# A two-layer decoder trunk on one core: the gate/up products with four of eight chunks by sevens, two of the sums on GpSimd

## The chip, the cores and the metric

The kernel runs on one NeuronCore of a Trainium2 chip. Its engines work side by side: TensorE (PE; its weight loads are listed as PEld), VectorE (DVE), ScalarE (ACT), GpSimd (POOL) and SyncE (SP, here only a queue that starts transfers). The metric is the device time of one execution in microseconds; the times given are medians of several runs.

## The reference

The input is x with 256 tokens of 2048 float32 channels. Two layers follow each other, each a token mixer and a feed-forward network, both behind an RMSNorm and both added to the stream:

```python
for i in range(DEPTH):                      # DEPTH = 2
    hn = rmsnorm(h, norm_mix[i])
    if i % N_MIXERS == 0:
        mix = pool_mixer(hn, pool_w[j], pool_scale[j])
    else:
        mix = diff_attention(hn, w_qkv[j], ..., w_o[j], lambda_init)
    h = h + mix
    h = h + swiglu(rmsnorm(h, norm_ffn[i]), w_gate[i], w_up[i], w_down[i])
return rmsnorm(h, final_norm)
```

The pooling mixer takes, in four groups of 512 channels, the mean over the last 2, 4, 8 or 16 tokens less the token itself, times a 512x512 matrix. The attention has 8 heads of two score maps each. `swiglu` is `(silu(h @ wg) * (h @ wu)) @ wd` with 5632 inner channels. Everything is float32, and nearly all of the arithmetic lies in the matrix products with the weights, 353 MB of which are read once.

## The kernel before

**Products in three terms.** A float32 product is made of fp32r matmuls: each operand is split into a high half (a cast) and a low half (what the cast left), and a product is high x high, high x low and low x high. For weights, `halves` (lines 111 to 116) casts on ScalarE (`whi`, L114) and subtracts on VectorE (`wlo`, L115). The activations are the stationary operand, 128x128; the weights are the moving one, 512 columns.

**A group.** `group` (lines 137 to 178) makes one product of the 256 tokens with 1024 columns of a weight matrix. It goes through the input channels in chunks of 256; a weight chunk is four blocks of 128x512 in one tile of 1 MB, loaded by `load` (L108, SyncE's queue, three buffers `raw`), split into three pairs of buffers `whi`/`wlo`. A chunk is a product of 2x2 blocks. Done plainly it has eight block products, 24 matmuls, into the four banks of the result. Done by sevens (Strassen's scheme in Winograd's form) it has seven block products, 21 matmuls, into seven banks, and needs sums of the blocks: `sums` (lines 118 to 124) makes T1 and T3 (L120), T2 (L122) and T4 (L123) on VectorE, `sum_halves` splits them on ScalarE (L129) and VectorE (L130). The tiles of the sums have one buffer each. Plain chunks of the same group add into the banks M2, P3, P4 and X, which are combined later.

**Which chunks go by sevens** is listed per stage: `SEVEN = (2, 4, 6)` for gate/up, `SEVEN_DOWN` for the down product, `SEVEN_QKV`, `SEVEN_O`. The first gate/up group of layer 0 takes only chunk 6. The eight PSUM banks are M1, M6, M7, P5, P3, P4, M2, X (0 to 7). `combined` (lines 180 to 197) makes the four result blocks out of them with two copies on ScalarE and eight additions on VectorE, the last of them reading X (L196).

**The feed-forward network** (`ffn`, lines 388 to 451) has 11 gate/up groups of eight chunks in three bundles (4, 4, 3); after each bundle come two down groups (8, 8 or 6 chunks) that add to `x_tok`. After a gate/up group come silu (L408), the product with up (L409), and `pair` (lines 230 to 253), which transposes the result on TensorE (L235) into an auxiliary bank, one of 0 to 3 in turn (`aux`), and splits it; where the pair feeds a chunk by sevens, it also makes the sums S1 to S4.

**The start** (lines 264 to 385): x is loaded in four pieces of 512 KB (two column halves for each half of the tokens), the four mixer weights and the band matrix behind them on SyncE's queue. For each group g, `turned` transposes and scales x (L310, L313, L315), `product` multiplies with the weights as full float32 (L322), `scaled_halves`, `means` and `residual` make the windowed means and add them, `onward` transposes the new stream for the next product.

**The end**: the last down group, all plain, is followed for each half of the tokens by the addition (L429), squares (L216), a product with the final gain (L435), 1/sqrt (`rsqrt`), scaling (L445, L446) and the output (L447).

**Order.** The order on each engine isn't that of the source: a scheduler of the framework puts every instruction where its operands and buffers are free by its own model of time; the waits between engines follow from it. So matmuls of the next group stand between the transposes of the last one. SyncE's queue starts its transfers one after another, and a load that waits for a buffer holds those behind it.

Of the kernel before, what the change touches and what calls it, by code (L numbers as in the profile page):

```python
# [30 lines left out]
BAND = 3 * P  # L31
LAMBDA_INIT = 0.8 - 0.6 * math.exp(-0.3)
# [6 lines left out]
SEVEN = (2, 4, 6)  # L39
# [12 lines left out]
def trunk_kernel(ctx, tc, x_n, gains, scale_in, final_in, subln, lam_in, band, dist,  # L52
# [31 lines left out]
    dist_sb = const.tile([P, 2 * P], F32, name="dist_sb")  # L84
    ident = const.tile([P, P], F32, name="ident")
    ones = const.tile([P, P], F32, name="ones")
    nc.vector.memset(ones, 1.0)
    make_identity(nc, ident)

# [28 lines left out]
    def sums(pool, raw):  # L118
        t = pool.tile([P, 4, 512], F32, name="tsum")
        nc.vector.tensor_tensor(t[:, T1:T3 + 1], raw[:, B11:B22 + 1],  # L120
                                raw[:, B12:B12 + 1].broadcast_to([P, 2, 512]), ALU.add)
        nc.vector.tensor_tensor(t[:, T2], t[:, T1], raw[:, B22], ALU.add)  # L122
        nc.vector.tensor_tensor(t[:, T4], t[:, T2], raw[:, B21], ALU.add)  # L123
        return t
# [12 lines left out]
    def group(steps, pool):  # L137


        plan = []  # L140
        for a, seven, src in steps:
            if seven:
                plan.append([(M1, [(A11, 0, B11)]), (M2, [(A12, 0, B21)]), (M6, [(S2, 1, T2)]), (M7, [(S3, 1, T3)]),
                             (P5, [(S1, 1, T1)]), (P3, [(S4, 0, B22)]), (P4, [(A22, 1, T4)])])
            else:
                plan.append([(C11, [((0, 0), 0, B11), ((1, 0), 0, B21)]), (C12, [((0, 0), 0, B12), ((1, 0), 0, B22)]),
                             (C21, [((0, 1), 0, B11), ((1, 1), 0, B21)]), (C22, [((0, 1), 0, B12), ((1, 1), 0, B22)])])
        left = {}
# [4 lines left out]
        for (a, seven, src), step in zip(steps, plan):  # L153
            raw = load(src)
            t = sums(pool, raw) if seven else None
            w = [halves(raw, B11 if seven else 0)]
            if seven:
                w.append(sum_halves(pool, t))
            for b, parts in step:
                first = b not in ps  # L160
                if first:
                    ps[b] = bank(b)
                for at, which, block in parts:
                    hi, lo = w[which]
                    if seven:
                        ah, al = a[:, 0, at], a[:, 1, at]
                    else:
                        k, t = at
                        if a.shape[2] == 8:
                            slot = ((A11, A21), (A12, A22))[k][t]  # L170
                            ah, al = a[:, 0, slot], a[:, 1, slot]
                        else:
                            ah, al = (a[:, k, i, t * P:(t + 1) * P] for i in range(2))
                    for x, y in ((ah, hi), (ah, lo), (al, hi)):
                        left[b] -= 1
                        nc.tensor.matmul(ps[b], x, y[:, block], start=first, stop=(left[b] == 0))  # L176
                        first = False
        return ps
# [51 lines left out]
    def pair(dst, src, gains, seven):  # L230

        ps = aux((P, 2, 2, P))
# [32 lines left out]
    with tc.tile_pool(name="start", bufs=1, reuse_waits="tile") as st:  # L265

        warm = tmp.tile([P, 8], F32, name="warm", bufs=1)
        nc.scalar.activation(warm[:, 0:1], ones[:, 0:1], AF.Sqrt)
# [4 lines left out]
        w_pool = [st.tile([P, 4, 512], F32, name=f"w{g}") for g in range(3)]  # L273
        scale_sb = st.tile([P, D], F32, name="scale_sb")
        band_raw = st.tile([P, 4 * BAND + 8], F32, name="band_raw")
        nc.scalar.dma_start(out=gain_sb, in_=gains)
        ss_in = tmp.tile([P, 2, 4], F32, name="ss")

        def load_x(i):
            cols = slice(i * 1024, (i + 1) * 1024)  # L280
            for t in range(2):
                nc.sync.dma_start(out=x_tok[:, t, cols], in_=x_n[:, t, cols])

        def squares(i):
            for t in range(2):
                sq = st.tile([P, 1024], F32, name="sq_in")
                nc.scalar.activation(sq, x_tok[:, t, i * 1024:(i + 1) * 1024], AF.Square, accum_out=ss_in[:, t, i:i + 1])
# [10 lines left out]
        counts = band_raw[:, 4 * BAND:].rearrange("p (g t) -> p g t", t=2)  # L298
        xt, yp, y, zp = {}, {}, {}, {}

        def turned(g):

            xt[g] = [st.tile([P, 2, S], F32, name="xt", bufs=6) for _ in range(2)]
            for i in range(2):
                ps = aux((P, 2, S))
                for k in range(2):
                    at = 2 * i + k
                    cols = slice((4 * g + at) * P, (4 * g + at + 1) * P)
                    for t in range(2):
                        nc.tensor.transpose(ps[:, k, t * P:(t + 1) * P], x_tok[:, t, cols], ident)  # L310
# [6 lines left out]
        def product(g):  # L317

            yp[g] = [bank(4 + 2 * (g % 2) + t) for t in range(2)]
            for at in range(4):  # L320
                for t in range(2):
                    nc.tensor.matmul(yp[g][t], xt[g][at // 2][:, at % 2, t * P:(t + 1) * P], w_pool[g][:, at],  # L322
                                     start=(at == 0), stop=(at == 3))
# [30 lines left out]
        turned(0)  # L354
        squares(0)
        turned(1)
        product(0)
        squares(1)
        tot = tmp.tile([P, 2], F32, name="ss_tot")
# [15 lines left out]
        product(3)  # L375
# [10 lines left out]
    nc.sync.dma_start(out=dist_sb, in_=dist)  # L386

    def ffn(layer, xq, ss, next_op, next_gain):
# [3 lines left out]
        with tc.tile_pool(name=f"ffn{layer}", bufs=1, reuse_waits="tile") as hp:  # L392
            g0 = 0
            ys = []
            for c, n in enumerate(CHUNKS):
# [6 lines left out]
                for g in range(g0, g0 + n):  # L402

                    by_seven = SEVEN[-1:] if g == 0 and layer == 0 else SEVEN
# [5 lines left out]
                    for i in range(2):  # L410
                        at = 2 * (g - g0) + i
                        ht = hp.tile(pair_shape(at in SEVEN_DOWN), F32R, name="h", tag=f"h{at}")
                        pair(ht, lambda k, t: cs[t][1][:, (2 * i + k) * P:(2 * i + k + 1) * P], None, at in SEVEN_DOWN)
                        hp_tiles.append(ht)
                for o in range(2):
                    if last and o == 1:
# [5 lines left out]
                    by_seven = () if last and o and next_op is None else SEVEN_DOWN  # L422
                    cs = combined(group([(hp_tiles[i], i in by_seven, w_down[layer][o, 2 * g0 + i])
                                         for i in range(2 * n)], hp), hp)
                    ends = last and o and next_op is None
                    for b, t in ((0, 0), (1, 0), (0, 1), (1, 1)) if ends else ((0, 0), (0, 1), (1, 0), (1, 1)):
# [5 lines left out]
                        if last and next_op is None:  # L432
                            if b == 0 and t == 0:
                                ys.append(hp.tile([P, 2, 2, 512], F32, name="y", tag=("tsum", "thi")[o]))
# [4 lines left out]
                        if ends and b:  # L439

                            tot = tmp.tile([P, 2], F32, name="ss_tot")
                            nc.vector.tensor_reduce(tot[:, 0:1], ss_next[:, t], AX.X, ALU.add)
                            rt = rsqrt(tot[:, 0:1], D, 1)
                            for i in range(2):
                                nc.scalar.activation(ys[i][:, t, 0], ys[i][:, t, 0], AF.Copy, scale=rt)  # L445
                                nc.vector.tensor_scalar(ys[i][:, t, 1], ys[i][:, t, 1], rt, None, ALU.mult)  # L446
                                (nc.scalar if i else nc.sync).dma_start(  # L447
                                    out=out[t * P:(t + 1) * P, i * 1024:(i + 1) * 1024],
                                    in_=ys[i][:, t].rearrange("p b n -> p (b n)"))
# [8 lines left out]
    with tc.tile_pool(name="attn", bufs=1, reuse_waits="tile") as ap_, ExitStack() as heads:  # L458
# [4 lines left out]
            small[:, a:b] for a, b in ((0, 2), (2, 4), (4, 8), (8, 10), (10, 12), (12, 13), (14, 16)))  # L463
        nc.sync.dma_start(out=subln_sb, in_=subln)
# [3 lines left out]

        nc.vector.tensor_tensor(lp, lam_sb[:, 0:2], lam_sb[:, 2:4], ALU.mult)
# [75 lines left out]
        for g in range(2):  # L545
            cs = scaled(combined(group([(xp[p], p in SEVEN_QKV, w_v[g, p]) for p in range(NP)], op_), op_), (r_col, r_col))
            for h in range(4 * g, 4 * g + 4):
# [13 lines left out]
                oT[h] = op_.tile(pair_shape(h in SEVEN_O), F32R, name=f"oT{h}")  # L561
# [33 lines left out]
def _constants():  # L595
# [14 lines left out]
    band = np.concatenate([band.reshape(P, -1), counts.reshape(P, -1)], axis=1)  # L610
# [50 lines left out]
```

## Time and profile before

| What | us |
|---|---|
| median of three runs (lowest, highest) | 1848.4 (1846.57, 1849.46) |
| the profiled execution, its own time | 1848.95 |
| its span in the trace | 1847.2 |
| ScalarE busy in the span | 1034.5 |
| VectorE busy in the span | 1595.1 |

The span runs from the first to the last recorded instruction or transfer; the 1.75 us around it are in the execution's time alone. Rows of groups read: line, engine, operation, result<-operands, shapes, count | busy us, mean ns | idle time before. In rows of stretches each engine has its busy time and, in brackets, its number of instructions; the granted TensorE clock, the share of the DMA engines and their GB/s end the row. Durations of successive VectorE instructions overlap by about 0.08 us, since a row's time includes its start-up; busy time counts the overlap once.

### The profile page before, as it was taken

Reading aid. Unit: us, or ns where it says so; the run is one execution under the profiler, and the core shown is the slowest. Engines: PE = TensorE matmul, PEld = TensorE weight load, DVE = VectorE, ACT = ScalarE, POOL = GpSimd, SP = SyncE. Lnnn points to the kernel's source line nnn. Section 1 sums busy time; section 2 is a strip of 40 time slices with the busy share of each in tenths; the row PEclk is TensorE's granted clock in tenths of the full one; section 3 lists DMA queues with packets and bytes.
Section 4 is the critical chain, followed back from the end, with each engine's and each line's share of the span. In section 5 each row is a group of like instructions: output and inputs, shape, how many; then the busy total and the mean of one; then the engine's idle time right before and its main releaser. Section 6 shows DMA issues by size and latency. Waiting matters only on the chain.

```text
span 1847.2 us, 20836 instructions
## 1 busy us (share of the span) xinstructions
PE 1832.2 (99%) x8194; PEld 1493.6 (81%) x8194; DVE 1595.1 (86%) x1644; ACT 1034.5 (56%) x998; POOL 0.7 (0%) x6
## 2 busy tenths in 40 slices
PE   9999999999999999999999999999999999999997
PEld 5888888888888888888888888788888888888886
DVE  5889998898989899988888678998989899988985
ACT  5655555555554556665566655555554555555553
POOL 0000000000000000000000000000000000000000
PEclk9999999999999999999999999999999999999999
DMA  6555555555555555555554454555555555566552
GB/s 256 198 193 194 186 212 196 208 200 192 203 198 205 202 186 182 206 181 175 170 179 160 162 193 169 208 202 188 203 201 205 197 190 190 211 217 210 197 198 99
DMA packets 50210, 356.74 MB, mean 193 GB/s; under 512 B 5952, under 2 KB 6080, under 8 KB 7488
## 3 DMA queue, kind: packets, MB, share of 16 engines
q1 hardware_dynamic: 49392, 353.27, 54.2%
q10 hardware_dynamic: 720, 2.15, 0.3%
q8 instruction: 64, 1.05, 0.2%
q14 instruction: 34, 0.28, 0.0%
HBM read 353.30 MB, written 2.10 MB: 192 GB/s over the span
## 4 chain that ended last, share of the span: by engine, by line
PE 94%; DVE 3%; DMA 1%; ACT 1%; issue 1%; SPq 0%; DVEq 0%; ACTq 0%
PE b L176 89%; PE b L235 2%; PE b L322 2%; DVE wlo L115 1%; PE b L506 1%; PE b L536 0%; DMA w<-pool_w 0%; ACT whi L114 0%; DMA raw<-w_v 0%; DMA raw<-w_gu 0%; DVE tsum L120 0%; DVE tlo L130 0%; PE b L310 0%; PE b L491 0%; ACT sq L216 0%
## 5 line engine op out<-in xcount | busy, mean ns | idle before, releaser
L176 PE MATMUL b<-whi,xp 128*128 128x512 f32 x2824 | 909.3, 392 | 1.0 <-DVE c L188 1.0
L114 ACT CAST whi<-raw 128x1536 fp32r<-128x1536 f32 (+1 forms) x328 | 581.3, 1773 | 583.1 <-PE b L176 498.7
L115 DVE TENSOR_TENSOR wlo<-raw,whi 128x1536 fp32r<-128x1536 f32 (+1 forms) x328 | 692.6, 2112 | 193.9 <-ACT whi L114 193.7
L176 PEld LDWEIGHTS b<-whi,xp 128*128 128x128 f32 x2824 | 528.3, 188 | 110.5 <-DVE c L188 1.4
L176 PE MATMUL b<-wlo,xp 128*128 128x512 f32 x1412 | 551.8, 391 | 0.0
L176 PE MATMUL b<-whi,h 128*128 128x512 f32 x1108 | 354.5, 390 | 0.0
L176 PEld LDWEIGHTS b<-wlo,xp 128*128 128x128 f32 x1412 | 265.3, 188 | 53.6
L130 DVE TENSOR_TENSOR tlo<-tsum,thi 128x2048 fp32r<-128x2048 f32 x108 | 246.8, 2285 | 5.8 <-ACT thi L129 5.8
L176 PEld LDWEIGHTS b<-whi,h 128*128 128x128 f32 x1108 | 207.4, 188 | 43.1
L176 PE MATMUL b<-wlo,h 128*128 128x512 f32 x554 | 215.8, 389 | 0.0
L129 ACT CAST thi<-tsum 128x2048 fp32r<-128x2048 f32 x108 | 206.2, 1909 | 16.7 <-DVE tsum L123 16.6
L176 PE MATMUL b<-thi,xp 128*128 128x512 f32 x608 | 211.8, 390 | 0.0
L120 DVE TENSOR_TENSOR tsum<-raw 128x1024 f32<-128x1024 f32 x108 | 131.8, 1220 | 2.6 <-DMA raw<-w_v 1.1
L176 PEld LDWEIGHTS b<-thi,xp 128*128 128x128 f32 x608 | 113.9, 188 | 24.1 <-ACT thi L129 0.9
L176 PEld LDWEIGHTS b<-wlo,h 128*128 128x128 f32 x554 | 104.0, 188 | 21.3
L176 PE MATMUL b<-tlo,xp 128*128 128x512 f32 x304 | 119.5, 393 | 0.0
L176 PE MATMUL b<-thi,h 128*128 128x512 f32 x240 | 83.7, 389 | 0.0
L123 DVE TENSOR_TENSOR tsum<-tsum,raw 128x512 f32<-128x512 f32 x108 | 74.3, 688 | 2.2
L122 DVE TENSOR_TENSOR tsum<-tsum,raw 128x512 f32<-128x512 f32 x108 | 74.0, 685 | 0.7
L176 PE MATMUL b<-whi,oT 128*128 128x512 f32 x236 | 74.4, 392 | 0.0
L176 PEld LDWEIGHTS b<-tlo,xp 128*128 128x128 f32 x304 | 57.0, 188 | 16.0 <-DVE tlo L130 4.4
L176 PEld LDWEIGHTS b<-thi,h 128*128 128x128 f32 x240 | 45.0, 188 | 9.2
(139 smaller groups left out, 1181.6 us busy)
## 6 DMA issues: line engine op xcount, KB each, us to landing
raw<-w_gu SPq DMA_DIRECT2D x176, 1024.0 KB, 4.9
raw<-w_down SPq DMA_DIRECT2D x88, 1024.0 KB, 4.9
raw<-w_qk SPq DMA_DIRECT2D x32, 1024.0 KB, 4.8
raw<-w_v SPq DMA_DIRECT2D x16, 1024.0 KB, 4.8
raw<-w_o SPq DMA_DIRECT2D x16, 1024.0 KB, 4.9
w<-pool_w SPq DMA_DIRECT2D x3, 1024.0 KB, 11.7
x_tok<-x_n SPq DMA_DIRECT2D x4, 512.0 KB, 6.1
scale_sb<-scale_in SPq DMA_DIRECT2D x1, 1024.0 KB, 13.1
```

The costliest lines, as they stand in the source:

```text
L114: nc.scalar.copy(hi[:, lo_block:], raw[:, lo_block:])
L115: nc.vector.tensor_tensor(lo[:, lo_block:], raw[:, lo_block:], f32(hi[:, lo_block:]), ALU.subtract)
L120: nc.vector.tensor_tensor(t[:, T1:T3 + 1], raw[:, B11:B22 + 1], raw[:, B12:B12 + 1].broadcast_to([P, 2, 512]), ALU.add)
L122: nc.vector.tensor_tensor(t[:, T2], t[:, T1], raw[:, B22], ALU.add)
L123: nc.vector.tensor_tensor(t[:, T4], t[:, T2], raw[:, B21], ALU.add)
L129: nc.scalar.copy(hi, t)
L130: nc.vector.tensor_tensor(lo, t, f32(hi), ALU.subtract)
L176: nc.tensor.matmul(ps[b], x, y[:, block], start=first, stop=(left[b] == 0))
L235: nc.tensor.transpose(ps[:, i, 1 - t if seven else t], src(i, t), ident)
L322: nc.tensor.matmul(yp[g][t], xt[g][at // 2][:, at % 2, t * P:(t + 1) * P], w_pool[g][:, at], start=(at == 0), stop=(at == 3))
L506: nc.tensor.matmul(sc[:, :nk], qk[:, 0, c, qb * P:(qb + 1) * P], qk[:, 1, c, :nk], start=True, stop=True)
```

## The change

- `SEVEN` becomes `(0, 2, 4, 6)`. Group 0 of layer 0 still has only chunk 6 by sevens and group 0 of layer 1 still 2, 4, 6; the other 20 gate/up groups have four.
- `sums` makes T2 and T4 on GpSimd, in every stage that uses sevens.
- The pairs of h are transposed into bank X, no longer into banks 0 to 3.
- The mixer loads x as the first 512 columns and the other 1536, and its first weights in two halves; its first product starts before the second transposition. The groups 2 and 3 multiply in three fp32r terms, with split x and split weights, in place of full float32. The band is loaded after the squares, into a buffer that it shares with them.
- The last down group makes its last two chunks bank by bank, and `finish` ends each half of the tokens on its own, in blocks of 256 columns where the last result comes in.
- `ones`, `dist_sb` and four of the attention's outputs `oT` lie in other buffers.

```diff
+PLAIN = 2
-SEVEN = (2, 4, 6)
+SEVEN = (0, 2, 4, 6)
...
-        nc.vector.tensor_tensor(t[:, T2], t[:, T1], raw[:, B22], ALU.add)
-        nc.vector.tensor_tensor(t[:, T4], t[:, T2], raw[:, B21], ALU.add)
+        nc.gpsimd.tensor_tensor(t[:, T2], t[:, T1], raw[:, B22], ALU.add)
+        nc.gpsimd.tensor_tensor(t[:, T4], t[:, T2], raw[:, B21], ALU.add)
...
-    def group(steps, pool):
+    def group(steps, pool, by_bank=0):
...
+        head = len(steps) - by_bank
+        for (a, seven, src), step in zip(steps[:head], plan[:head]):
+            w = prepared(seven, src)
             for b, parts in step:
...
+                products(a, seven, w, b, parts)
+        if by_bank:
+            ws = [prepared(seven, src) for a, seven, src in steps[head:]]
+            for n in range(len(plan[head])):
+                for (a, seven, src), step, w in zip(steps[head:], plan[head:], ws):
+                    products(a, seven, w, *step[n])
         return ps
...
-    def pair(dst, src, gains, seven):
-        ps = aux((P, 2, 2, P))
+    def pair(dst, src, gains, seven, at=None):
+        ps = aux((P, 2, 2, P)) if at is None else bank(at, (P, 2, 2, P))
...
+        parts = slice(0, 512), slice(512, D)
...
         load_x(0)
-        nc.sync.dma_start(out=w_pool[0], in_=pool_w[0])
+        for i in range(2):
+            nc.sync.dma_start(out=w_pool[0][:, 2 * i:2 * i + 2], in_=pool_w[0, :, 2 * i:2 * i + 2])
         load_x(1)
-        nc.sync.dma_start(out=band_raw, in_=band)
         nc.sync.dma_start(out=w_pool[1], in_=pool_w[1])
+        w_pool.append(load(pool_w[2]))
+        w_pool.append(load(pool_w[3]))
         nc.sync.dma_start(out=scale_sb, in_=scale_in)
-        nc.sync.dma_start(out=w_pool[2], in_=pool_w[2])
-        w_pool.append(load(pool_w[3]))
...
-                    if g < 2:
+                    if g < PLAIN:
                         nc.vector.tensor_scalar(xt[g][i][:, k], ps[:, k], gain, None, ALU.mult)
                     else:
-                        nc.scalar.activation(xt[g][i][:, k], ps[:, k], AF.Copy, scale=gain)
+                        split(xt[g][i][:, k], ps[:, k], gain)
...
         turned(0)
+        product(0, (0, 1, 2))
         squares(0)
         turned(1)
-        product(0)
+        product(0, (3,))
         squares(1)
+        band_raw = st.tile([P, 4 * BAND + P], F32, name="wide", tag="wide")
+        nc.sync.dma_start(out=band_raw, in_=band)
...
+    def finish(cs, ys, final_sb, ss):
+        for t in range(2):
...
+            for b in range(2):
+                for h in range(2):
...
+                    nc.vector.tensor_tensor(x_tok[:, t, cols], cs[t][b][:, mine], x_tok[:, t, cols], ALU.add)
...
+                    nc.scalar.activation(sq[:, :S], x_tok[:, t, cols], AF.Square, accum_out=part[:, at:at + 1])
...
+                nc.vector.tensor_tensor(ys[1][:, t, b], x_tok[:, t, cols], final_sb[1][:, b * 512:(b + 1) * 512], ALU.mult)
...
+            rt = rsqrt(tot[:, 0:1], D, 1)
+            rows = slice(t * P, (t + 1) * P)
+            nc.scalar.activation(ys[1][:, t, 0], ys[1][:, t, 0], AF.Copy, scale=rt)
+            nc.scalar.dma_start(out=out[rows, 1024:1536], in_=ys[1][:, t, 0])
+            for b in range(2):
+                nc.vector.tensor_scalar(ys[0][:, t, b], ys[0][:, t, b], rt, None, ALU.mult)
+            nc.sync.dma_start(out=out[rows, 0:1024], in_=ys[0][:, t].rearrange("p b n -> p (b n)"))
+            nc.vector.tensor_scalar(ys[1][:, t, 1], ys[1][:, t, 1], rt, None, ALU.mult)
+            nc.sync.dma_start(out=out[rows, 1536:2048], in_=ys[1][:, t, 1])
...
-                    by_seven = SEVEN[-1:] if g == 0 and layer == 0 else SEVEN
+                    by_seven = SEVEN if g else SEVEN[1:] if layer else SEVEN[-1:]
...
-                        pair(ht, lambda k, t: cs[t][1][:, (2 * i + k) * P:(2 * i + k + 1) * P], None, at in SEVEN_DOWN)
+                        pair(ht, lambda k, t: cs[t][1][:, (2 * i + k) * P:(2 * i + k + 1) * P], None, at in SEVEN_DOWN, X)
...
-                oT[h] = op_.tile(pair_shape(h in SEVEN_O), F32R, name=f"oT{h}")
+                if h < 4:
+                    oT[h] = op_.tile(pair_shape(h in SEVEN_O), F32R, name=f"oT{h}")
+                else:
+                    oT[h] = resid.tile(pair_shape(h in SEVEN_O), F32R, name="xp", tag=f"xp{h}")
```

More of the change, by code (lines that the diff above doesn't have):

```diff
@@ L83, in trunk_kernel @@
     gain_sb = const.tile([P, 6, NK], F32, name="gain_sb")
-    dist_sb = const.tile([P, 2 * P], F32, name="dist_sb")
     ident = const.tile([P, P], F32, name="ident")
-    ones = const.tile([P, P], F32, name="ones")
-    nc.vector.memset(ones, 1.0)
-    make_identity(nc, ident)
     x_tok = resid.tile([P, 2, D], F32, name="x_tok")
@@ L152, in group, with prepared @@
         ps = {}
-        for (a, seven, src), step in zip(steps, plan):
+        def prepared(seven, src):
             raw = load(src)
@@ L158, in group, with products @@
                 w.append(sum_halves(pool, t))
-            for b, parts in step:
[L160 to L177, printed above, removed]
+            return w
+        def products(a, seven, w, b, parts):
+            first = b not in ps
+            if first:
+                ps[b] = bank(b)
+            for at, which, block in parts:
+                hi, lo = w[which]
+                if seven:
+                    ah, al = a[:, 0, at], a[:, 1, at]
+                else:
+                    k, t = at
+                    if a.shape[2] == 8:
+                        slot = ((A11, A21), (A12, A22))[k][t]
+                        ah, al = a[:, 0, slot], a[:, 1, slot]
+                    else:
+                        ah, al = (a[:, k, i, t * P:(t + 1) * P] for i in range(2))
+                for x, y in ((ah, hi), (ah, lo), (al, hi)):
+                    left[b] -= 1
+                    nc.tensor.matmul(ps[b], x, y[:, block], start=first, stop=(left[b] == 0))
+                    first = False
+        head = len(steps) - by_bank
+        for (a, seven, src), step in zip(steps[:head], plan[:head]):
+            w = prepared(seven, src)
+            for b, parts in step:
+                products(a, seven, w, b, parts)
[4 more added lines that the diff above has]
+                    products(a, seven, w, *step[n])
         return ps
@@ L265, in trunk_kernel @@
     with tc.tile_pool(name="start", bufs=1, reuse_waits="tile") as st:
+        ones = st.tile([P, P], F32, name="ones")
+        nc.vector.memset(ones, 1.0)
         warm = tmp.tile([P, 8], F32, name="warm", bufs=1)
+        make_identity(nc, ident)
         nc.scalar.activation(warm[:, 0:1], ones[:, 0:1], AF.Sqrt)
@@ L311, in turned, with product @@
                     gain = gain_sb[:, 0, 4 * g + at:4 * g + at + 1]
-                    if g < 2:
+                    if g < PLAIN:
                         nc.vector.tensor_scalar(xt[g][i][:, k], ps[:, k], gain, None, ALU.mult)
                     else:
-                        nc.scalar.activation(xt[g][i][:, k], ps[:, k], AF.Copy, scale=gain)
-        def product(g):
-            yp[g] = [bank(4 + 2 * (g % 2) + t) for t in range(2)]
-            for at in range(4):
-                for t in range(2):
-                    nc.tensor.matmul(yp[g][t], xt[g][at // 2][:, at % 2, t * P:(t + 1) * P], w_pool[g][:, at],
-                                     start=(at == 0), stop=(at == 3))
+                        split(xt[g][i][:, k], ps[:, k], gain)
+        def product(g, some):
+            if some[0] == 0:
+                yp[g] = [bank(4 + 2 * (g % 2) + t) for t in range(2)]
+                if g >= PLAIN:
+                    w_pool[g] = halves(w_pool[g])
+            for at in some:
+                for t in range(2):
+                    a, w, rows = xt[g][at // 2][:, at % 2], w_pool[g], slice(t * P, (t + 1) * P)
+                    if g < PLAIN:
+                        nc.tensor.matmul(yp[g][t], a[:, rows], w[:, at], start=(at == 0), stop=(at == 3))
+                        continue
+                    for j, (u, v) in enumerate(((a[:, 0, rows], w[0]), (a[:, 0, rows], w[1]), (a[:, 1, rows], w[0]))):
+                        nc.tensor.matmul(yp[g][t], u, v[:, at], start=(at == 0 and j == 0), stop=(at == 3 and j == 2))
         def scaled_halves(g):
@@ L374, in trunk_kernel @@
         onward(0)
-        product(3)
+        product(3, (0, 1, 2, 3))
         scaled_halves(2)
@@ L433, in ffn @@
                             if b == 0 and t == 0:
-                                ys.append(hp.tile([P, 2, 2, 512], F32, name="y", tag=("tsum", "thi")[o]))
+                                ys.append([hp.tile([P, 2, 2, 512], F32, name="y", tag=("tsum", "thi")[i]) for i in range(2)])
+                                ys = ys[0]
                             nc.vector.tensor_tensor(ys[o][:, t, b], x_tok[:, t, cols],
@@ L438, in ffn @@
                             transposed(next_op, j, next_gain, SEVEN_QKV)
[L439 to L449, printed above, removed]
                 g0 += n
@@ L463, in trunk_kernel @@
             small[:, a:b] for a, b in ((0, 2), (2, 4), (4, 8), (8, 10), (10, 12), (12, 13), (14, 16)))
+        dist_sb = hq.tile([P, 2 * P], F32, name="dist_sb")
+        nc.sync.dma_start(out=dist_sb, in_=dist)
         nc.sync.dma_start(out=subln_sb, in_=subln)
@@ L467, in trunk_kernel @@
         nc.vector.tensor_scalar(qs_col, r_col, QK_SCALE, None, ALU.mult)
+        ones = hq.tile([P, P], F32, name="ones")
+        nc.vector.memset(ones, 1.0)
         nc.vector.tensor_tensor(lp, lam_sb[:, 0:2], lam_sb[:, 2:4], ALU.mult)
@@ L609, in _constants @@
         band[:, g, 2] = full[:P, P:]
-    band = np.concatenate([band.reshape(P, -1), counts.reshape(P, -1)], axis=1)
+    band = np.concatenate([band.reshape(P, -1), counts.reshape(P, -1), np.zeros((P, P - 8), np.float32)], axis=1)
     q, k = np.arange(P)[:, None], np.arange(P)[None, :]
```

47 lines of the change are left out of this document (31 added, 16 removed).

## The prediction

> **What bounds the kernel now.** I read the page's busy shares and its chain first, then a table of stretches, then the groups of one gate/up group.
>
> ```profile
> span 1847.2 us, 20836 instructions
> PE 1832.2 (99%) x8194; PEld 1493.6 (81%) x8194; DVE 1595.1 (86%) x1644; ACT 1034.5 (56%) x998; POOL 0.7 (0%) x6
> ...
> PE 94%; DVE 3%; DMA 1%; ACT 1%; issue 1%; SPq 0%; DVEq 0%; ACTq 0%
> PE b L176 89%; PE b L235 2%; PE b L322 2%; DVE wlo L115 1%; PE b L506 1%; PE b L536 0%; DMA w<-pool_w 0%; ACT whi L114 0%; DMA raw<-w_v 0%; DMA raw<-w_gu 0%; DVE tsum L120 0%; DVE tlo L130 0%; PE b L310 0%; PE b L491 0%; ACT sq L216 0%
> ```
>
> TensorE is busy for 99% and the chain of work that ended last runs through it for 94%, nearly all of it the matmuls of `group` (L176). So an edit counts if it takes matmuls away and no other engine becomes the bound. That condition is read from one steady gate/up group. Columns of the stretches: length, then busy time of PE, PEld, DVE, ACT, POOL.
>
> ```profile
> 140.69 41.38 PE b L176 x181
> 226.13 124.33 PE b L176 x547
> ...
> 140.03:182.75 42.72, 42.72 (x194) 35.02 (x192) 38.84 (x37) 24.17 (x19) 0.00 (x0) 1.00 0.57 197
> ```
>
> 547 matmuls in 124.33 us make **0.2273 us per matmul**. Group 140.03 to 182.75 lasts 42.72 us with no hole in PE, while DVE works 38.84 (91%) and ACT 24.17. PE is the bound, and DVE is 3.9 us behind it. The DVE rows of that group (count | busy, mean ns | idle before):
>
> ```profile
> L115 DVE TENSOR_TENSOR wlo<-raw,whi 128x2048 fp32r<-128x2048 f32 x5 | 11.4, 2289 | 3.7 <-ACT whi L114 3.7
> L115 DVE TENSOR_TENSOR wlo<-raw,whi 128x1536 fp32r<-128x1536 f32 x4 | 7.0, 1752 | 0.0
> L130 DVE TENSOR_TENSOR tlo<-tsum,thi 128x2048 fp32r<-128x2048 f32 x3 | 6.9, 2285 | 0.0
> L120 DVE TENSOR_TENSOR tsum<-raw 128x1024 f32<-128x1024 f32 x3 | 3.7, 1219 | 0.0
> L122 DVE TENSOR_TENSOR tsum<-tsum,raw 128x512 f32<-128x512 f32 x4 | 2.7, 686 | 0.0
> L123 DVE TENSOR_TENSOR tsum<-tsum,raw 128x512 f32<-128x512 f32 x3 | 2.1, 689 | 0.1
> ...
> L187 DVE TENSOR_TENSOR c<-b,c 128x512 f32<-128x512 f32 x1 | 0.7, 685 | 0.0
> ```
>
> DVE's only idle time, 3.7 us, is a wait for ACT's `whi`, and ACT's own waits are nearly all for PE:
>
> ```profile
> ACT whi L114 <- PE b L176: 498.7, 225, 4.7
> DVE wlo L115 <- ACT whi L114: 193.7, 146, 4.2
> ```
>
> So the halves are made as far ahead as the three buffers allow, then wait for PE to free one: 498.7/225 = 2.2 us of slack each time.
>
> **The change, part by part.** *Gate/up by sevens.* A plain chunk costs 24 matmuls, one by sevens 21. Group 0 of each layer keeps its number of sevens; 20 groups go from three to four. PE saves 20 x 3 x 0.2273 = **13.6 us**, if PE remains the bound: a group falls from 42.72 to 42.04 us.
>
> What DVE pays: a fourth seven adds L120, L130 and the short L115 and takes away a long L115: 1.22 + 2.29 + 1.75 - 2.29 = 2.97 us. The three sevens that were there lose L122 and L123: 3 x (0.686 + 0.689) = 4.1 by durations; successive ones start some 0.08 us before the last ends, so 3.7. DVE comes to 38.84 + 2.97 - 3.7 = **38.1 of 42.04 us**, again 91%.
>
> ```profile
> L114 ACT CAST whi<-raw 128x2048 fp32r<-128x2048 f32 x220 | 421.0, 1914 | 376.7 <-PE b L176 343.7 <-ACT h L239 18.4 <-issue 4.8
> L129 ACT CAST thi<-tsum 128x2048 fp32r<-128x2048 f32 x108 | 206.2, 1909 | 16.7 <-DVE tsum L123 16.6
> L114 ACT CAST whi<-raw 128x1536 fp32r<-128x1536 f32 x108 | 160.4, 1485 | 206.4 <-PE b L176 155.1 <-DVE c L194 33.7 <-issue 16.8
> ```
>
> ACT gains 1.91 + 1.49 - 1.91 = 1.5 us, 25.7 of 42: hidden by its 18 us of idle time.
>
> *The two sums on GpSimd.* The trace has no such operation; the nearest are at the start:
>
> ```profile
> masks.py:199 POOL TENSOR_SCALAR_AFFINE_SELECT ident<-ident 128x128 f32<-128x128 f32 x1 | 0.3, 294 | 0.1
> masks.py:197 POOL MEMSET ident<- 128x128 f32 x1 | 0.2, 205 | 0.3 <-POOLq L652 0.3
> L652 POOL MEMSET const-float32-1.0<- 128x1 f32 x1 | 0.1, 99 | 0.0
> ```
>
> Low end: the MEMSET's growth, (205-99)/127 = 0.83 ns per element, gives 0.52 us for 512. High end: AFFINE_SELECT's growth of 1.54 ns for one input, doubled for two: 1.67 us. I take four times the 294 ns of AFFINE_SELECT, 1.18 us, as that row reads SBUF and computes. The eight sums of a group fill 9.4 of 42 us on an engine that does nothing else. Their chain T2, T4 is 2 x (1.18 - 0.69) = 1 us longer, within the 2.2 us of slack. As price for DVE I take nothing; the other end is that DVE stands still while GpSimd works (first rival). The Trainium skill ("GPSIMD Engine Reference", Elementwise — side-by-side cycle accounting) has 4497 ns for 2048 elements; a quarter, an estimate, is 1.12 us; by it the forecast stays and the first rival gives 1897. No row here shows it.
>
> *The h transposes in bank X.* By sevens, the next group's first chunk uses seven banks at once and X only in its second chunk.
>
> ```profile
> 178.98 0.68 DVE L193 TENSOR_TENSOR c<-b,c 128x512 f32<-128x512 f32 x1
> ...
> 180.18 0.68 DVE L196 TENSOR_TENSOR c<-b,c 128x512 f32<-128x512 f32 x1
> ...
> 181.90 0.38 PE L235 MATMUL b<-ident,c 128*128 128x128 f32 x2
> ...
> 182.58 0.82 PE L235 MATMUL b<-ident,c 128*128 128x128 f32 x6
> ...
> 184.71 0.68 DVE L240 TENSOR_TENSOR h<-b,h 128x512 fp32r<-128x512 f32 x1
> ```
>
> X is read for the last time at 180.18 (L196), the transposes run at 181.9 to 183.4, their copies to 185.4. With both pairs in one bank the second follows the copies of the first, some 1.5 us later: X is free near 187. L193 (first combined result out of a bank that the next chunk writes) waited for the group's last matmuls until 178.98; the new second chunk writes X 21 + 18 matmuls later, 178.98 + 8.9 = 187.8. Just free: cost 0. Before a down group, whose first chunk is plain, X is wanted after 18 matmuls, at 183.1; PE then needs 4 us of other matmuls, which the next two chunks offer. If they aren't ready: 6 such places, up to 4 us each, **+24** at worst. I take +2.
>
> *Edges.* Combining (eight instructions of 0.68 us) now falls beside a chunk by sevens, not two plain ones: 5.2 instead of 2.3 us of DVE work per chunk. The buffered halves cover one such step; where they don't, a group loses up to the 0.68 us that it won, 0 to +14 in all. I take +1.
>
> *Mixer.*
>
> ```profile
> 1.65 6.92 DMA w<-pool_w
> ...
> 8.62 1.13 PE b L322 x2
> ...
> 28.99 6.87 PE b L322 x16
> ...
> 0.00:10.00 10.00, 7.27 (x31) 6.01 (x32) 1.52 (x4) 3.91 (x7) 0.70 (x6) 0.98 0.83 316
> ...
> 20.00:30.00 10.00, 9.99 (x35) 5.37 (x34) 3.50 (x6) 4.46 (x10) 0.00 (x0) 1.00 0.72 299
> 30.00:40.00 10.00, 10.00 (x33) 5.37 (x32) 7.16 (x11) 7.58 (x13) 0.00 (x0) 1.00 0.30 104
> 40.00:50.00 10.00, 10.00 (x41) 6.44 (x40) 10.00 (x15) 7.00 (x15) 0.00 (x0) 1.00 0.53 183
> ...
> L228 DVE SCALAR_TENSOR_TENSOR xp<-b,gain_sb,xp 128x256 fp32r<-128x256 f32 x32 | 14.4, 477 | 0.2 <-ACT xp L227 0.2
> ```
>
> The first product waits until 8.6 us for x (1 MB) and w (1 MB). With x in 512 columns and w in halves, 1 MB suffices: at the 316 GB/s of this stretch some 3 us sooner, 2.7 taken. Groups 2 and 3 take 24 matmuls of 0.2273 = 5.46 us instead of 6.87: -2.8. Against it DVE gets two `wlo` (4.6), eight splits of `xt` (8 x 0.48 by L228, of that shape; 3.8) and 1.2 for the larger xq[0]: 9.6 us. It has 9.3 idle us from 20 to 40, none from 40 to 50. The band now waits behind the squares and lands later. Ends -5.5 and +4; I take **-3**.
>
> *Tail.*
>
> ```profile
> 1835.91 0.39 PE L176 MATMUL b<-whi,h 128*128 128x512 f32 x1
> ...
> 1837.90 0.16 DVE L442 TENSOR_REDUCE ss_tot<-ss 128x1 f32<-128x4 f32 x1
> ...
> 1839.93 0.88 DVE L446 TENSOR_SCALAR y<-y,rs_r 128x512 f32<-128x512 f32 x2
> ...
> 1841.79 0.35 ACTq L447 DMA_DIRECT2D out_t<-y  x1
> GB/s 0 0 0 0 0 0 0 0 0 0 0 0 0 355 410 423 437 396 382 410 451 396 423 437 423 273 423 437 437 410 68 27 0 0 0 0 0 0 0 0
> ```
>
> From the last matmul's end (1836.3) to the span's end are 10.9 us: 1.6 to the sum of squares, 2.0 of 1/sqrt disturbed by the other half's rows, 1.8 of scaling, 5.4 of output. Bank by bank, rows 0 to 127 are finished before the last matmul; the chain after it is 1.5 + 1.3 + 1.4, and 1 MB instead of 2 remains to be written at about 420 GB/s. I take **-2.5**, between 0 and -4.5.
>
> Sum: -13.6 + 2 + 1 - 3 - 2.5 = -16.1. The profiled execution took 1848.95 us (span 1847.2 and 1.75 around it), 0.55 above the median. 1848.95 - 16.1 = 1832.9, so **1832** against the median. The remaining edits (places of ones, dist and oT, a shared tile) issue the same work; cost 0, as PE's queue doesn't wait for them.
>
> **The rivals.** *GpSimd blocks DVE* (slower). A sum on GpSimd reads SBUF while DVE subtracts two SBUF tiles. If one stands still while the other runs, DVE is free for GpSimd only in its idle time (3.9) and in instructions that read a PSUM bank (L187, L188, L189, L193, L194, L196 and the plain h copy: seven at the 0.60 us from start to start of L193 to L196, 4.2), 8 of 42 us. Of 8 x 1.18 = 9.4 us, 80% then fall on DVE: 38.1 + 7.6 = 45.7 us per group, 3.7 above PE. 20 x 3.7 = 74: **1906**. It decides from 0.62 us per sum; at 0.75 the gain is gone; 0.9 gives 1868, 1.67 about 1967, 0.52 no loss. For it: nine tenths of DVE's time is two-input work. Against it: no row shows the two engines together. Down groups have one seven fewer and keep room. The Trainium skill ("SBUF — State Buffer", Who interferes with whom) says just this: a VectorE instruction with two SBUF inputs contends with a GpSimd instruction that reads SBUF, and whoever comes second blocks fully. By that rule this rival is the outcome; no run here shows it yet.
>
> *The gain is eaten at the edges.* X late before down groups, DVE crowded beside the combining, T2/T4 late for ACT's `thi`: +14 or more, mixer without gain: **1846**, from 1838 to 1856. For it: DVE is 91% full. Against: 498.7 us of buffer waits.
>
> *Only sevens count.* Mixer and tail give nothing: 1838, inside the forecast.
>
> **How the numbers follow.** PE remains the bound: 0.50, own range 1823 to 1842, all faster. Eaten at the edges: 0.18, of which 0.08 faster, 0.05 the same, 0.05 slower. GpSimd blocks DVE: 0.32, of which 0.02 the same, 0.30 slower. Faster 0.58, same 0.07, slower 0.35 (0.2%, 3.7 us, is what can be told from no change). The range takes in the lower two thirds of the blocking case: 1822 to 1900; some 0.12 lie above and 0.04 below.
>
> **What would show it.** Right: 8150 matmul records (60 fewer, 16 more in the mixer), steady gate/up groups of 42.0 us, PE without holes, L115 and L130 at 2.29 us as before, POOL near 300 us, the last matmul some 8.5 us before the end. Wrong: L115 or L130 longer or spread while POOL is busy, holes in PE ahead of `thi`/`tlo` matmuls, groups of 44 us or more; or holes ahead of the transposes.

## The result

The changed kernel takes 2013.39 us (median; 2003.82 to 2016.34), the kernel before 1848.38. The ratio is 1.0884 (95% interval 1.0872 to 1.0897): 165 us slower, where 16 us faster were forecast, and outside the range of 1822 to 1900.

### The profile page after: what moved, and what is told of

It reads as the page before. It is cut to its first block, busy times and chain, and to the rows that moved or that the text cites. A ratio compares the mean times of both kernels' runs of the same rounds, so it can differ in the third digit from the quotient of the medians.

```text
span 2013.2 us, 21180 instructions
## 1 busy us (share of the span) xinstructions
PE 1881.7 (93%) x8150; PEld 1509.1 (75%) x8150; DVE 1624.7 (81%) x1491; ACT 1064.3 (53%) x1028; POOL 544.3 (27%) x262
## 5 line engine op out<-in xcount | busy, mean ns | idle before, releaser
L175 PE MATMUL b<-whi,xp 128*128 128x512 f32 x2732 | 899.7, 396 | 21.4 <-DVE h L250 21.4
L111 DVE TENSOR_TENSOR wlo<-raw,whi 128x1536 fp32r<-128x1536 f32 (+1 forms) x330 | 716.5, 2174 | 228.1 <-ACT whi L110 228.1
L118 POOL TENSOR_TENSOR tsum<-tsum,raw 128x512 f32<-128x512 f32 x128 | 310.8, 2428 | 1397.9 <-DVE tsum L116 515.8
L125 ACT CAST thi<-tsum 128x2048 fp32r<-128x2048 f32 x128 | 244.3, 1909 | 234.1 <-POOL tsum L119 234.0
L126 DVE TENSOR_TENSOR tlo<-tsum,thi 128x2048 fp32r<-128x2048 f32 x128 | 292.4, 2284 | 89.2 <-ACT thi L125 89.2
L175 PE MATMUL b<-thi,xp 128*128 128x512 f32 x784 | 299.3, 420 | 31.5 <-ACT thi L125 27.9
L119 POOL TENSOR_TENSOR tsum<-tsum,raw 128x512 f32<-128x512 f32 x128 | 232.8, 1819 | 10.0
L175 PEld LDWEIGHTS b<-thi,xp 128*128 128x128 f32 x784 | 157.4, 204 | 70.6 <-ACT thi L125 35.9
L175 PE MATMUL b<-tlo,xp 128*128 128x512 f32 x392 | 169.1, 431 | 33.6 <-DVE tlo L126 33.6
L116 DVE TENSOR_TENSOR tsum<-raw 128x1024 f32<-128x1024 f32 x128 | 156.1, 1219 | 3.4 <-DMA raw<-w_v 0.7
L175 PEld LDWEIGHTS b<-tlo,xp 128*128 128x128 f32 x392 | 80.7, 206 | 63.7 <-DVE tlo L126 47.5
L200 ACT COPY c<-b 128x512 f32<-128x512 f32 x41 | 24.1, 589 | 53.2 <-PE b L175 53.2
```

Of the source, the lines that this page charges most:

```text
L111: nc.vector.tensor_tensor(lo[:, lo_block:], raw[:, lo_block:], f32(hi[:, lo_block:]), ALU.subtract)
L118: nc.gpsimd.tensor_tensor(t[:, T2], t[:, T1], raw[:, B22], ALU.add)
L119: nc.gpsimd.tensor_tensor(t[:, T4], t[:, T2], raw[:, B21], ALU.add)
L125: nc.scalar.copy(hi, t)
L126: nc.vector.tensor_tensor(lo, t, f32(hi), ALU.subtract)
L200: nc.scalar.copy(p5, ps[P5])
```

## The profile after

The page's first lines and its groups of the two sums (L118 is T2, L119 is T4) and of the cast behind them:

```profile
span 2013.2 us, 21180 instructions
PE 1881.7 (93%) x8150; PEld 1509.1 (75%) x8150; DVE 1624.7 (81%) x1491; ACT 1064.3 (53%) x1028; POOL 544.3 (27%) x262
...
L118 POOL TENSOR_TENSOR tsum<-tsum,raw 128x512 f32<-128x512 f32 x128 | 310.8, 2428 | 1397.9 <-DVE tsum L116 515.8
...
L125 ACT CAST thi<-tsum 128x2048 fp32r<-128x2048 f32 x128 | 244.3, 1909 | 234.1 <-POOL tsum L119 234.0
...
L119 POOL TENSOR_TENSOR tsum<-tsum,raw 128x512 f32<-128x512 f32 x128 | 232.8, 1819 | 10.0
```

PE has 8150 matmul records, as forecast, and yet is busy 49.5 us longer than in the kernel before, and idle for 131.5 us where it was idle for 15. VectorE isn't busier by share: 81% of the span against 86%. GpSimd, forecast near 300 us, is busy for 544. The two sums take 2428 and 1819 ns on average, and ScalarE's cast `thi` (L125) waits 234 us for the second.

One steady gate/up group (between two silu of successive groups, as for the kernel before) in the table of stretches, and the waits in it (who waited for whom: us, times, longest):

```profile
192.90:241.65 48.75, 44.63 (x190) 35.63 (x191) 40.84 (x31) 26.05 (x21) 17.32 (x8) 0.96 0.46 167
ACT thi L125 <- POOL tsum L119: 9.0, 4, 5.1
DVE wlo L111 <- ACT whi L110: 6.1, 3, 2.4
PEld b L175 <- DVE tlo L126: 2.0, 2, 1.8
```

The group lasts 48.75 us, not 42.0. VectorE works for 40.84 of them, 2.7 more than forecast, but still less than the 42.0 that PE needs: VectorE isn't full. It waits for ScalarE (6.1), which waits for GpSimd (9.0): the chain of sums is late, and the casts that stand behind `thi` in ScalarE's order wait with it.

What a sum on GpSimd meets is seen in the timeline (start us, us, engine, line). First GpSimd, then VectorE in the same 6 us:

```profile
182.73 2.69 POOL L118 TENSOR_TENSOR tsum<-tsum,raw 128x512 f32<-128x512 f32 x1 [5.75 <-ACT c L196]
185.50 1.30 POOL L119 TENSOR_TENSOR tsum<-tsum,raw 128x512 f32<-128x512 f32 x1
```

```profile
182.51 1.75 DVE L111 TENSOR_TENSOR wlo<-raw,whi 128x1536 fp32r<-128x1536 f32 x1
184.18 0.68 DVE L197 TENSOR_TENSOR c<-b,c 128x512 f32<-128x512 f32 x1
184.97 0.69 DVE L199 TENSOR_TENSOR c<-b,c 128x512 f32<-128x512 f32 x1
185.76 1.58 DVE L201 TENSOR_TENSOR c<-c,c 128x512 f32<-128x512 f32 x1
```

The first sum starts at 182.73 while `wlo` (two SBUF tiles) runs, and ends at 185.42, 1.16 us after `wlo`. A sum alone takes 1.27 us (below), so this one stood still until about the end of `wlo`. L197 and L199, which read one PSUM bank and one SBUF tile, run beside GpSimd at their usual 0.68. L201, two SBUF tiles, starts at 185.76 during the second sum and takes 1.58 us instead of 0.68: it stood still for about as long as GpSimd ran, to 186.80. So each side holds the other back, one instruction at a time. The shortest sum, undisturbed, takes 1.27 us, as the range of its rows shows (ns: shortest, median, longest):

```profile
L118 POOL TENSOR_TENSOR tsum<-tsum,raw x128: 1272/2692/3444, 69.3 to 1949.2; 128x512 f32<-128x512 f32 x128
```

VectorE's long subtractions over the whole kernel:

```profile
L111 DVE TENSOR_TENSOR wlo<-raw,whi 128x2048 fp32r<-128x2048 f32 x202 | 489.3, 2423 | 202.6 <-ACT whi L110 202.6
L126 DVE TENSOR_TENSOR tlo<-tsum,thi 128x2048 fp32r<-128x2048 f32 x128 | 292.4, 2284 | 89.2 <-ACT thi L125 89.2
```

`wlo` takes 2423 ns on average instead of 2289. `tlo` keeps its length: it comes only after the two sums, and the next sum waits for it, since the tiles of the sums have one buffer. Over all 128 chunks by sevens, T2 starts 0.12 to 0.14 us after T1 has ended, so the hop to GpSimd is short. T4 ends 4.46 us after T1 on average and 2.75 at best: the two sums alone make 2.75, and 1.71 is time in which they stand still.

What that does to PE, twenty microseconds later (in brackets the idle time before, and for whom):

```profile
204.28 0.39 PE L175 MATMUL b<-whi,xp 128*128 128x512 f32 x1
205.97 0.97 PE L175 MATMUL b<-thi,xp 128*128 128x512 f32 x3 [1.30 <-ACT thi L125]
208.30 0.80 PE L175 MATMUL b<-tlo,xp 128*128 128x512 f32 x1 [1.36 <-DVE tlo L126]
208.89 0.63 PE L175 MATMUL b<-thi,xp 128*128 128x512 f32 x1
209.32 0.63 PE L175 MATMUL b<-tlo,xp 128*128 128x512 f32 x1
...
211.82 0.40 PE L175 MATMUL b<-whi,xp 128*128 128x512 f32 x1
```

PE waits for `thi` and then for `tlo`, and after the second hole its matmuls start 0.43 us apart instead of 0.23, for 3 us, with a granted clock of 0.50 from 208.3 to 211.7: here a late sum is paid twice. Late loads are no part of this: GpSimd also reads the weights that the next load overwrites, but ScalarE waits only 6.8 us in all for gate/up weights.

## The experiments

Theory A: reads of SBUF by GpSimd and two-input instructions of VectorE hold each other back. Its rivals: B, the fourth seven crowds at a group's edge; C, bank X; D, any hop over GpSimd is too late. Within A: A1, the sums come late; A2, VectorE loses time.

**Sums back on VectorE.**

```diff
-        nc.gpsimd.tensor_tensor(t[:, T2], t[:, T1], raw[:, B22], ALU.add)
-        nc.gpsimd.tensor_tensor(t[:, T4], t[:, T2], raw[:, B21], ALU.add)
+        nc.vector.tensor_tensor(t[:, T2], t[:, T1], raw[:, B22], ALU.add)
+        nc.vector.tensor_tensor(t[:, T4], t[:, T2], raw[:, B21], ALU.add)
```

> The changed kernel with T2 and T4 back on VectorE; nothing else is undone. Theory A (each sum on GpSimd waits for a two-input VectorE instruction and holds back the next one, so thi comes late, PE stands still and then runs at a lower clock): most of the 165 us goes, 1850 to 1885 us; what stays above the kernel before is the h pair in bank X (six waits of about 4 us) and VectorE, which has 43 us of work per gate/up group against 42.0 of PE. Theory B (a fourth seven, whose sums, halves and combining crowd at a group's edge, is what PE waits for, wherever T2 and T4 are made): above 1950 us. Theory C (bank X): within 20 us of the changed kernel.

Measured: 1892.64 us, ratio 1.0242 (1.0225 to 1.0259). 121 of the 165 us are gone, so most is due to GpSimd; the time itself lies 8 us above the expected range. A steady group in the table of stretches:

```profile
139.52:185.28 45.76, 43.68 (x190) 34.08 (x189) 43.05 (x40) 25.61 (x20) 0.00 (x0) 1.00 0.51 184
```

VectorE has 43.05 us of work, as worked out beforehand, but the group lasts 45.76: at 94% of VectorE there is little room for a wait. Four sevens don't fit with all sums on VectorE; three do (42.72). ScalarE also waits 108.2 us for loads of gate/up weights here, against 2.6 in the run with start and end only; why was not tried. The six waits for bank X don't occur. VectorE is busy for 1689.8 us in this run, 65 more than in the changed kernel, which is 121 us slower: so VectorE's busy time is not what the changed kernel loses most by.

**The kernel before with the two sums on GpSimd**, the same two lines the other way.

> The kernel before with one edit: T2 and T4 on GpSimd. Theory A: 108 chunks by sevens take part, three in a gate/up group, so slower by 50 to 110 us (1900 to 1960). Theory B and theory C: VectorE is relieved by 3.7 us per gate/up group and PE stays the bound, 1840 to 1855 us.

Measured: 1899.88 us, ratio 1.0281 (1.0265 to 1.0296). This edit alone costs 51 us, at the low end of A's estimate, although VectorE does 1.37 us less per seven and is busy for 1523.5 us instead of 1595.1. The loss is waiting, not VectorE's work: PE is idle for 53.7 us instead of 15.0, and ScalarE's `thi` waits 122.2 us for the second sum, where it waited 16.6 us for VectorE's. Not all of it falls on gate/up groups: from the silu of layer 0's last group to that of layer 1's first, a stretch with the attention, the time grows by 21.1 us.

**The h transposes in banks 0 to 3** in the changed kernel.

```diff
-  pair(ht, ..., None, at in SEVEN_DOWN, X)
+  pair(ht, ..., None, at in SEVEN_DOWN)
```

> The changed kernel with the h transposes in banks 0 to 3 again. Theory C: bank X is the main cause, below 1930 us. Theory A: only the six waits ahead of the down groups can go, 21 us and some lost clock behind them, but banks 0 to 3 are now wanted at once by the next chunk by sevens; between 1980 and 2020 us.

Measured: 2018.33 us, ratio 1.0921 (1.0901 to 1.0942). The six waits went, and the waits for `tlo` and `thi` took their place. PE's waits of the changed kernel, then of this one:

```profile
PE b L175 <- DVE tlo L126: 35.4, 26, 1.8
PE b L175 <- ACT thi L125: 28.1, 19, 3.2
PE b L175 <- DVE h L250: 21.4, 6, 3.6
```

```profile
PE b L175 <- DVE tlo L126: 49.7, 41, 1.8
PE b L175 <- ACT thi L125: 38.7, 32, 3.2
```

Theory C falls.

**Start and end only**: three sevens, sums on VectorE, h in banks 0 to 3.

```diff
-SEVEN = (0, 2, 4, 6)
+SEVEN = (2, 4, 6)
-                    by_seven = SEVEN if g else SEVEN[1:] if layer else SEVEN[-1:]
+                    by_seven = SEVEN if g or layer else SEVEN[-1:]
```

(with the edits of the first and third runs)

> The changed kernel with three sevens per gate/up group, T2 and T4 on VectorE and the h transposes in banks 0 to 3: what is left of the change is the mixer, the end and the places of tiles. By the terms of the prediction -3 and -2.5: 1843 us, between 1838 and 1850. If the start or the end is part of the loss: above 1855.

Measured: 1845.53 us, ratio 0.9983 (0.9973 to 0.9992), the only kernel with the full computation that is faster than both, by 0.2% against the kernel before. The last matmul's row and the span:

```profile
span 1844.2 us, 20902 instructions
...
1834.66 0.39 PE L175 MATMUL b<-whi,h 128*128 128x512 f32 x1
```

The last matmul ends at 1835.05 (before: 1836.30), the span 9.15 us later (10.9): the start and all between gained 1.25 us, the end 1.75. These are single executions, and those of the kernel before differ by up to 4 us.

**T2 and T4 only written.**

```diff
-        nc.gpsimd.tensor_tensor(t[:, T2], t[:, T1], raw[:, B22], ALU.add)
-        nc.gpsimd.tensor_tensor(t[:, T4], t[:, T2], raw[:, B21], ALU.add)
+        nc.gpsimd.memset(t[:, T2], 0.5)
+        nc.gpsimd.memset(t[:, T4], 0.5)
```

> The changed kernel, but GpSimd only writes T2 and T4 (a constant, no operand read): both sums are left out of the computation. It takes away the reading of SBUF by GpSimd and most of the length of the chain, and leaves the hops to GpSimd and back, the four sevens and bank X. Theory A (reads of GpSimd and two-input VectorE instructions hold each other back): the rows of POOL about 0.5 us each, VectorE rows as before, VectorE 38.1 of 42.0 us per gate/up group, time 1832 plus the six waits for bank X, 1832 to 1862 us. Theory D (any hop over GpSimd is too late for ScalarE): above 1900 us.

Measured: 1830.36 us, ratio 0.9900 (0.9883 to 0.9916). POOL's rows and a steady group:

```profile
L119 POOL MEMSET tsum<- 128x512 f32 x128 | 68.2, 533 | 0.0
L118 POOL MEMSET tsum<- 128x512 f32 x128 | 67.5, 527 | 1634.4 <-DVE tlo L126 1603.5 <-PE b L340 16.6 <-PE b L175 14.3
```

```profile
137.50:179.37 41.87, 41.87 (x189) 34.32 (x189) 38.13 (x32) 25.46 (x22) 3.99 (x8) 1.00 0.58 200
```

Here is the timetable of the forecast: 41.87 us per group without a hole, VectorE 38.13, clock 1.00. VectorE's `wlo` is back at 2290 ns. B falls as far as the edges go. Theory D falls only in part: a constant needs neither T1 nor the weights, and the idle row shows that GpSimd writes it as soon as the last `tlo` is done, long ahead. So this run takes away two things at once, the reads and the way from T1 over GpSimd to ScalarE. That this way is too long even without reads is neither shown nor ruled out. Against this run, whose PE records are the same 8150, the changed kernel's span of 2013.2 is 184.2 us longer than 1829.0; PE's busy time there is 1813.0. So 115.5 us are holes and 68.7 us are longer rows of the same matmuls. The mean clock is 0.973 against 0.998, which accounts for some 47 of these (an estimate, 1813.0 x 0.998 / 0.973 less 1813.0).

**The same with h in banks 0 to 3.**

> As the run before (T2 and T4 only written, the sums left out), with the h transposes in banks 0 to 3. Theory C in small (bank X costs its six waits, 21 us and some clock): 20 to 30 us below the run before. Rival: in banks 0 to 3 the next chunk by sevens waits instead, within 8 us of it or above.

Measured: 1834.41 us, ratio 0.9923 (0.9908 to 0.9938). Without late sums bank X is 4 us better than banks 0 to 3; the changed kernel's six waits there came with the late sums, not from the bank alone.

**Idle sums.** To the kernel with start and end only, after T4:

```diff
+        for _ in range(2):
+            spare = tmp.tile([P, 512], F32, name="spare", bufs=1)
+            nc.gpsimd.tensor_tensor(spare, raw[:, B22], raw[:, B21], ALU.add)
```

> The kernel of the third pair of edits (start and end only, three sevens, all sums on VectorE, 1845.5 us) with two additional sums of 512 columns per chunk by sevens on GpSimd, into a tile that nothing reads: the same reads of SBUF, but nobody waits for them. Theory A1 (what costs is that the sums come late): POOL rows up to 2.4 us as in the changed kernel, VectorE loses about 0.4 us per sum, 2.4 us of the 3.9 that it has free per gate/up group, within 15 us of 1845. Theory A2 (what costs is VectorE's time, 80% of 6 x 1.3 us per gate/up group): VectorE reaches 45 us per group, 1890 to 1910 us.

Measured: 1940.73 us, ratio 1.0496 (1.0480 to 1.0512): 95 us above the kernel without them, though nothing waits for these sums. The steady group without and with them:

```profile
136.58:179.33 42.75, 42.75 (x192) 35.01 (x191) 38.86 (x36) 24.17 (x19) 0.00 (x0) 1.00 0.56 197
```

```profile
137.77:182.94 45.17, 43.30 (x193) 34.91 (x191) 42.83 (x36) 24.18 (x19) 11.80 (x6) 1.00 0.53 187
```

Six sums put 3.97 us on VectorE, 0.66 us each, and the group grows from 42.75 to 45.17. A1 as the only cause falls: reads that nobody needs cost time. The group's length is A2's 45 us, but VectorE works for 42.83 of them, not 45: it was charged about 1.0 us per sum and lost 0.66. VectorE's own T2 and T4 grow from 0.69 to 0.93 us, and `thi` waits for them 87.9 us instead of 13.7, so sums come late here too. The total is 31 us above A2's range, since I had charged gate/up groups alone: from silu to silu, two down groups and the gate/up group behind them take 134.1 us instead of 125.7, and the stretch with the attention 518.6 instead of 497.0.

**Bank X in the kernel before.**

```diff
-        ps = aux((P, 2, 2, P))
+        ps = aux((P, 2, 2, P)) if at is None else bank(at, (P, 2, 2, P))
...
-  pair(ht, ..., None, at in SEVEN_DOWN)
+  pair(ht, ..., None, at in SEVEN_DOWN, X)
```

> The kernel before with one edit: the h transposes in bank X. All chunks 0 are plain here, so X is wanted 18 matmuls after each group's end. Theory C in small: PE stands still up to 4 us after each of the 22 gate/up groups, 1870 to 1930 us. Rival (the order is arranged around it): within 8 us of 1848.

Measured: 1863.88 us, ratio 1.0082 (1.0067 to 1.0097), between the two: the bank suits a group that begins by sevens and costs 15 us where the next begins plainly. It isn't by waits of up to 4 us: of PE's waits only that for a combined result grew, from 1.0 to 6.8 us in all, at most 0.8 at a time. How the rest arises wasn't tried.

**Sums of raw blocks alone.**

```diff
-        nc.gpsimd.tensor_tensor(t[:, T2], t[:, T1], raw[:, B22], ALU.add)
-        nc.gpsimd.tensor_tensor(t[:, T4], t[:, T2], raw[:, B21], ALU.add)
+        nc.gpsimd.tensor_tensor(t[:, T2], raw[:, B11], raw[:, B22], ALU.add)
+        nc.gpsimd.tensor_tensor(t[:, T4], raw[:, B12], raw[:, B21], ALU.add)
```

> The changed kernel, with GpSimd's two sums of the same size taken of raw blocks alone (B11+B22 and B12+B21 in place of T1+B22 and T2+B21; the sums are not those of the scheme). They read SBUF as much, but wait for no VectorE instruction and not for each other, so they can be made as soon as the weights have landed. Theory A2 (what costs is VectorE's time alone): it loses 8 x 0.66 us per gate/up group, as measured with the idle sums, 43.4 us and above for a group of 42.0; if that is the whole loss, the time stays near the changed kernel's, above 1980. Theory A1 (most of it is that the chain T1, T2, T4, thi, tlo comes late): only VectorE's loss is left, 1860 to 1915 us.

Measured: 1951.41 us, ratio 1.0549 (1.0531 to 1.0568), outside both ranges and between them. Two groups:

```profile
138.75:184.04 45.29, 42.72 (x188) 34.13 (x188) 44.17 (x32) 25.64 (x21) 20.77 (x8) 1.00 0.52 186
184.04:230.32 46.28, 43.03 (x190) 34.44 (x191) 43.72 (x31) 26.18 (x22) 19.79 (x8) 1.00 0.49 176
```

VectorE has 44 of 45 to 46 us: here it is nearly full. Between the written constants (1830) and the changed kernel (2013) lie 183 us; this run stands 121 above the one and 62 below the other. That is no split of the changed kernel's loss into A2 and A1. First, VectorE's busy time is 150.6 us above that with constants here (1685.7 against 1535.1), and only 89.6 in the changed kernel. Second, the sums are late here too, as they wait for the last `tlo` and stand still:

```profile
POOL tsum L118 <- DVE tlo L126: 668.2, 92, 21.4
ACT thi L125 <- POOL tsum L119: 127.4, 57, 9.0
```

In the changed kernel `thi` waits 234.0 us for them. So both A1 and A2 are at work, and how much each has of the 165 us stays open.

**Copies.**

```diff
+        nc.gpsimd.tensor_copy(t[:, T2], raw[:, B22])
+        nc.gpsimd.tensor_copy(t[:, T4], raw[:, B21])
```

(in place of the two sums)

> As the run before, but GpSimd copies one block each (B22 and B21; both sums are left out): one operand is read, not two. If any read of SBUF by GpSimd holds VectorE's two-input instructions back and is held back by them: POOL rows with a spread of over 2 us, VectorE's rows longer, 1836 to 1890 us. If only the two-operand form does: rows of one length and 1826 to 1834 us as with the written constants.

Measured: 1862.38 us, ratio 1.0077 (1.0058 to 1.0096); the first copy's rows:

```profile
L118 POOL COPY tsum<-raw x128: 613/1671/5421, 68.5 to 1794.3; 128x512 f32<-128x512 f32 x128
```

One operand is enough: 0.61 us undisturbed, 1.67 in the middle, up to 5.4. VectorE's short `wlo` (128x1536) grows from 1755 to 1962 ns. The price is 32 us above the written constants, against 121 for two operands.

## Why the prediction was wrong, point by point

**The step that failed** is the pricing of the two sums on GpSimd, in two sentences. The first is "As price for DVE I take nothing". In the changed kernel VectorE's busy time is 89.6 us above that of the run with written constants (1624.7 against 1535.1), 0.35 us per sum and 2.7 us per gate/up group; in the run with idle sums it is 0.66 per sum. The second is that their chain is 1 us longer, "within the 2.2 us of slack". GpSimd stands still as well: 2.43 and 1.82 us per sum instead of 1.18 make the chain 1.9 us longer than worked out. And the 2.2 us were the slack of another cast: `whi` waits for PE, while `thi`, which needs the sums, waited for T4 already in the kernel before (the row of L129 has 16.6 us). In the changed kernel it waits 234.0.

That the second sentence cost more is argued, from two numbers. VectorE's 40.84 us still fit into the 42.0 of a group, and with all sums on VectorE, where it works 65 us more, the kernel is 121 us faster. How much of the lateness is standing still, and how much is that two sums in a row on GpSimd are slow even undisturbed (2.75 us against 1.44 at best on VectorE), is open, as no run has the chain without the reads. An estimate from the timeline: taking from each of `thi`'s waits what its two sums took beyond 1.27 us each leaves some 114 of the 234 us.

**The rival that GpSimd blocks DVE** had 0.32. Its mechanism is what the runs show; its result, VectorE as the bound, is not. Against it stood only "no row shows the two engines together". That is no evidence, and the rule cited beside it (the Trainium skill, "SBUF — State Buffer", Who interferes with whom) said what the timeline now shows: whoever comes second waits for the whole instruction, and a VectorE instruction with at most one SBUF input, outside of its two-port modes, does not contend. The trace agrees on both: L201 1.58 instead of 0.68 us, L197 beside it 0.68. One more kind is held back in the trace: L570 in the attention, one SBUF tile times a column of scalars, takes up to 1.27 us beside a sum, and at most 0.37 in the run with constants; in which mode it runs, the trace doesn't say. With VectorE at 91%, most of it two-input work, that rule deserved the larger chance.

The rival's price was also too small: 1906, up to 1967 at 1.67 us per sum. Its term per group, 45.7 us, is close to the run with unchained sums (45.3 to 46.3), but the changed kernel's group lasts 48.75. It left out, first, the late chain. Second, the lower clock behind PE's holes, some 47 us. Third, the other stages: "Down groups have one seven fewer and keep room" doesn't hold, since two down groups and the gate/up group behind them take 135.3 us instead of 126.0 with constants, 9.3 more where a gate/up group alone takes 6.9 more; the stretch with the attention takes 27.7 more.

**Gate/up by sevens: right, but for that step.** With sums that are only written, a group takes 41.87 us (forecast 42.04), VectorE 38.13 (38.1), and the kernel 1830.4 (1832). That the total comes so close is partly luck: against the run with start and end only, sevens, bank and edges give 15.2 us (10.6 forecast), and start and end give 3.4 (5.5). Where the fourth seven's sums stay on VectorE, the kernel is 44 us slower than before: it hangs on a place for the two sums.

**One sum on GpSimd**: 1.18 us taken, 1.27 measured undisturbed; right in size, but only for a sum that nothing disturbs.

**Bank X and the edges**: +2 and +1 were taken. With written constants PE doesn't wait for the transposes or their copies. The worst case, 6 x 4 us, did occur in the changed kernel (21.4 us), with the late sums; with constants, or with the sums on VectorE, the same bank has none.

**Mixer and end**: right in sign, smaller in size: -1.25 for -3 (the first silu comes 0.97 us earlier) and -1.75 for -2.5.

## What to carry to other kernels

Before work is moved from VectorE to GpSimd, count how much of VectorE's time reads two SBUF tiles: there VectorE pays back half or all of what it saves (here 0.35 to 0.66 us per sum for 0.69 saved), and both sides come late. Then look at the one instruction that needs the result, and at its own slack, not at that of its neighbours. What GpSimd only wrote, and what ran beside VectorE's reads of PSUM, cost nothing here. Where a trace shows nothing of a resource that a change begins to share, the bound from that side is a case with a large chance, not a footnote.

## What the runs showed of the hardware

- A GpSimd sum of 512 columns takes 1.27 us undisturbed, a copy 0.61, a constant written 0.53. A row of POOL or VectorE here includes the time for which it stood still (L201 1.58 us, the sum at 182.73 2.69): it is seen as a longer row, not as idle time.
- Two holes in PE of 1.30 and 1.36 us within 4 us were followed by 3 us of matmuls 0.43 us apart (granted clock 0.50), but not always. The same pair earlier in the changed kernel, in the timeline, and the group it lies in, in the table of stretches:

```profile
156.61 0.96 PE L175 MATMUL b<-thi,xp 128*128 128x512 f32 x3 [1.32 <-ACT thi L125]
158.94 0.50 PE L175 MATMUL b<-tlo,xp 128*128 128x512 f32 x1 [1.36 <-DVE tlo L126]
159.28 0.40 PE L175 MATMUL b<-thi,xp 128*128 128x512 f32 x1
159.52 0.40 PE L175 MATMUL b<-tlo,xp 128*128 128x512 f32 x1
```

```profile
143.54:192.90 49.36, 43.30 (x188) 34.06 (x188) 41.73 (x32) 25.51 (x21) 20.33 (x8) 1.00 0.47 170
```

Here the matmuls go on 0.24 us apart and the clock of the group reads 1.00. What decides between the two was not tried.
